# Two layers of a hybrid decoder on one core: value blocks that run ahead of a way down are convolved and gated inside it, and the FFN's short part is the last but one

## The chip, the cores and the metric

The kernel runs on one core of a Trainium2 chip. A core has five engines with instruction queues of their own, which meet only at semaphores: TensorE (PE) multiplies matrices, VectorE (DVE) and GpSimd (POOL) do elementwise work on two operands, ScalarE (ACT) does elementwise functions of one operand and issues some DMAs, SyncE (SP) issues DMAs. Each engine takes its queue strictly in the order in which it is written. Sums of products build up in PSUM, everything else lies in SBUF. The metric is the device time of one execution in microseconds (us).

## The reference

One inference step runs 512 prompt tokens and 8 x 4 sample tokens (544 columns in all) through two layers of width 1024: an even mixer (attention and linear attention), a ConvFFN, an odd mixer (short gated convolution), a ConvFFN. The change is in the ConvFFN, whose hidden width is 2816:

```python
def conv_ffn(h, w_up, conv_w, conv_b, w_down, past):
    u = h @ w_up                                   # 1024 -> 2 x 2816
    uc, new = causal_dwconv(u, past, conv_w)       # 3 taps along time
    gate, val = jnp.split(uc + conv_b, 2, axis=-1)
    return (jax.nn.gelu(gate, approximate=True) * val) @ w_down, new

# around every sub-layer f:
x = x + rmsnorm(f(rmsnorm(x, g_pre)), g_post)
```

Inputs and outputs are float32; the last two rows of `u` per sequence (`new`) are outputs too.

## The kernel before, in words

All activations lie transposed, features on partitions and the 544 tokens along the free axis, in two halves of 256 and 288 columns. For precision each product uses a weight W = wh + wl and an operand x = xh + xl and issues three matmuls, wh.xh, wh.xl and wl.xh (`mm3`, lines 280, 285, 287). Weights come as units of 128 x 512 floats by DMA on SP's queue; ACT rounds a unit to wh (L199) and DVE, in one place POOL, subtracts for wl (L203). Ten buffers hold wh and ten wl; eleven hold raw units. PSUM has five banks (`pg`) for the large products and three (`px`) for small ones.

**The FFN.** The 2816 hidden features are 22 gate blocks c and 22 value blocks FC + c of 128. Blocks 0 to 4 ("raw") are multiplied before the norm is known and scaled as they leave PSUM; block 5 is "plain"; blocks 6 to 21 come in `pair(c)` by a scheme of seven products for eight, whose weight sums POOL's accumulating DMAs make (L252, L256). When a block of u is complete, `conv(c)` saves the state rows (POOL), applies the taps (ACT L1702, DVE L1703 and L1704) and, for a gate, the gelu (ACT L1706); for a value block it multiplies by the gate (DVE L1711) and splits the product into `gh` (ACT L514) and `gl` (DVE L515), the operands of the way down.

**The way down** multiplies a run of blocks by `ffn_down` into eight output blocks m. `PARTS` lists the runs, and `ffn_order` sets them between the up-products: a way down starts when one block more than it uses has been multiplied ("runs ahead"), so that block's convolution and gating is issued ahead of it. With PARTS (4, 4, 4, 4, 4, 2) the order is raw 0-4, down 0-3, plain 5, pairs 6-8, down 4-7, pairs 9-12, down 8-11, pairs 13-16, down 12-15, pairs 17-21, down 16-19, down 20-21. Each result leaves PSUM in `Post.ev`: in the first way down ACT copies it to m (L592), later DVE adds it to m (L594). All but the last go block by block, both halves of a block together (`seq(8)`); the last does all first halves, then all second halves (`ALL8`), and squares each finished half (ACT L522, L526; sums on POOL, the eighth on DVE, L527). With the sum complete, `finish` computes the norm factor (PE L378, DVE L382, POOL L383, PE L390, ACT L393), scales m (L639), adds it to the residual (L643) and makes xh (ACT L645) and xl (DVE L653, L655) for the next layer; in the last layer `Final` writes the outputs instead, with transposes on PE (L181) and the norm factor late (PE L762, DVE L765, POOL L766, DVE L777).

**Work inside a way down.** `run` calls `tick` after each group, which takes one item off the list `work`. In the first way down the items are `normal(k)`, k = 0 to 3: they write the normed input xn (DVE L1724), split it into xh (ACT) and xl (DVE) for the later blocks, and form 16 sums of quarters on POOL (L1743 to L1746). `out_states` transposes the state rows (PE L181), copies them (ACT L1832) and writes them by DMAs on ACT's queue (L1834, L1836), at the start of the last way down.

The order in which each engine's instructions stand is set by a scheduler from the program's order and its own estimates, within the dependencies.

Of the kernel before, what the change touches and what calls it, by code (L numbers as in the profile page):

```python
# [29 lines left out]
F = 2816  # L30
FC = F // P
C2 = 2 * FC
PARTS = (4, 4, 4, 4, 4, 2)
RAW, PLAIN = 5, 6
UN = 4 * P
MID = T // 2
# [52 lines left out]
def tile_hybrid_step(  # L89
# [1559 lines left out]
    def odd_rows():  # L1649
        stT = cpool.tile([P, NB * 2 * 8], F32, tag="scT", name="scT")  # L1650
        to_cols(stT, *load_rows([(state_conv[0].rearrange("n i (c p) -> (n i c) p", p=P), P)]))
        early["odd"] = stT

    def ffn(l, xh, xl, bc, post):
# [8 lines left out]

        us = {}
        gs = {}

        def smp(t):
            return t[:, TP + 2 : TP + 2 + 6 * NB].rearrange("p (n k) -> p n k", k=6)

        def tv(t, t0=TP):  # L1670
            return t[:, t0 : t0 + TS].rearrange("p (n t) -> p n t", t=NT)

        def open_u(c):
            u = us[c] = tt(w=AW, s="u")
# [4 lines left out]
        def ev(c, scaled=True):  # L1679
            def f(hf, ps):  # L1680
                u = us[c] if c in us else open_u(c)
                if not scaled:
                    t0, n = HALF[hf]
                    S.activation(u[:, 2 + t0 : 258 + t0], ps[:, 0:256], AF.Copy)
                    if hf == 1:
                        S.activation(smp(u)[:, :, 2:6], tv(ps, 256), AF.Copy)
                        conv(c)
                    return
                if hf == 0:
                    V.tensor_tensor(u[:, 2:258], ps[:, 0:256], bc[:, 0:256], ALU.mult)  # L1690
                    return
                V.tensor_tensor(u[:, 258:514], ps[:, 0:256], bc[:, 256:512], ALU.mult)
                V.tensor_tensor(smp(u)[:, :, 2:6], tv(ps, 256), tv(bc), ALU.mult)
                conv(c)

            return f

# [63 lines left out]
        def pair(c):  # L1761

            h = slice(0, MID)
            pa, pb, pc, pd = bank(), bank(), bank(), bank()
            p1, p5, u2, u3 = ht(), ht(), ht(), ht()
            ua, ub = open_u(c), open_u(FC + c)
            product(pa, xq["11"], True)
            S.activation(p1[:, h], pa[:, h], AF.Copy)
            product(pb, xq["t2"], True)
            V.tensor_tensor(u2[:, h], p1[:, h], pb[:, h], ALU.subtract)  # L1770
            product(pc, xq["t1"], True)
            S.activation(p5[:, h], pc[:, h], AF.Copy)  # L1772
            product(pa, xq["21"], False)
            S.activation(ua[:, 2 : 2 + MID], pa[:, h], AF.Copy)
            product(pb, xq["t3"], False)
            V.tensor_tensor(u3[:, h], pb[:, h], p1[:, h], ALU.subtract)
            product(pc, xq["22"], False)
            n = TP - MID
            V.tensor_tensor(ua[:, 2 + MID : 2 + TP], pc[:, :n], u2[:, :n], ALU.add)
            V.tensor_tensor(smp(ua)[:, :, 2:6], tv(pc, n), tv(u2, n), ALU.add)  # L1780
            conv(c)
            product(pd, xq["t4"], True)
            G.tensor_tensor(ub[:, 2 + MID : 2 + TP], u3[:, :n], p5[:, :n], ALU.subtract)
            G.tensor_tensor(smp(ub)[:, :, 2:6], tv(u3, n), tv(p5, n), ALU.subtract)  # L1784
            V.tensor_tensor(ub[:, 2 : 2 + MID], u3[:, h], pd[:, h], ALU.subtract)
            conv(FC + c)

        work = []

        def tick():  # L1790
            if work:
# [2 lines left out]
        for kind, c0, n in ffn_order():  # L1794
            if kind == "raw":
                jobs = []
                for c in range(c0, c0 + n):
                    jobs += [(8, xh, xl, ev(c)), (8, xh, xl, ev(FC + c))]
                run(jobs, FIRST4 + seq(len(jobs) - 5, 5), spare=SPARE)
                work += [lambda k=k: normal(k) for k in range(4)]  # L1800
            elif kind == "plain":
                work += [lambda i=i: (parts(i), parts(i + 1), parts(i + 2)) for i in (0, 3)]
                run([(8, xh, xl, ev(c, False)) for c in (c0, FC + c0)], seq(2), tick=tick)
                for k in range(4):
                    last_operand(k)
            elif kind == "pair":
                pair(c0)
            else:
                last = c0 + n == FC
                gh = [gs[c][0] for c in range(c0, c0 + n)]  # L1810
                gl = [gs[c][1] for c in range(c0, c0 + n)]
                if last:
                    out_states(uc, ffn_p[l, 0].rearrange("i (c p) -> (i c) p", p=P),
                               ffn_s[l].rearrange("n i (c p) -> (n i c) p", p=P), 2 * C2)
                    if isinstance(post, Final):
                        post.begin()
                    else:
                        odd_rows()
                jobs = [(n, gh, gl, post.ev(m, c0 == 0, last)) for m in range(8)]
                run(jobs, ALL8 if last else seq(8), tick=tick)  # L1820

# [169 lines left out]
```

## Time and profile before

| | us |
|---|---|
| runs | 1351.59, 1348.55, 1353.99 (median 1351.59) |
| profiled execution: its own time | 1346.55 |
| its span in the trace | 1344.8 |
| PE busy | 1263.1 (94%), 9710 matmuls |
| DVE / ACT / POOL busy | 967.9 / 683.6 / 448.5 |

Times in the trace count from the span's start. Matmuls are pipelined, so a matmul of 0.28 us starts some 0.12 us after the one before it. A row of a timeline ends with the idle time before the instruction and what released it, in brackets, where the engine was idle. Idle time of an engine counts only where the end of the program hangs on it.

### The profile page before, as it was taken

What the parts mean: (1) busy time and instruction counts of PE and PEld (TensorE: products, weight loads), DVE (VectorE), ACT (ScalarE), POOL (GpSimd) and SP (SyncE); (2) the same over time, 40 slices, a digit from 0 to 9 for tenths busy, and PEclk for the clock granted to TensorE, in tenths of its full rate; (3) what the DMA queues carried; (4) which work ended last, traced back from release to release, by engine and by line L of the source; (5) the groups of instructions that cost most, each with busy time, mean ns of one, the idle gap of its engine ahead of it and who ended that gap; (6) DMA issues with size and microseconds to landing.
All of it is one profiled execution on the core that took longest, in us unless ns stands there. A gap on an engine that the chain in (4) does not pass through costs nothing.

```text
span 1344.8 us, 26495 instructions
## 1 busy us (share of the span) xinstructions
PE 1263.1 (94%) x9710; PEld 1222.5 (91%) x9710; DVE 967.9 (72%) x1958; ACT 683.6 (51%) x1489; POOL 448.5 (33%) x700
## 2 busy tenths in 40 slices
PE   8999989989899999989987999998979999999997
PEld 7999867889899999989977999998979999999996
DVE  7586465488959687878948655528886978787976
ACT  7554564655556364636634322335555646463634
POOL 4100210062463344445243100025254535353613
PEclk9999999999989999999988999999989999999998
DMA  8512220323657989989621332321456799989902
GB/s 255 128 47 61 86 71 10 89 64 97 130 105 185 185 195 185 219 173 219 173 66 32 111 90 86 92 79 32 131 114 140 182 194 205 193 197 196 214 8 74
DMA packets 311884, 171.98 MB, mean 128 GB/s; under 512 B 20829, under 2 KB 301882, under 8 KB 311738
## 3 DMA queue, kind: packets, MB, share of 16 engines
q1 hardware_dynamic: 262914, 132.17, 34.3%
q0 software_dynamic: 43456, 34.74, 18.1%
q10 hardware_dynamic: 5384, 3.38, 0.8%
q8 instruction: 76, 1.25, 0.4%
q14 instruction: 54, 0.44, 0.1%
HBM read 149.01 MB, written 5.47 MB: 115 GB/s over the span
## 4 chain that ended last, share of the span: by engine, by line
PE 70%; DMA 11%; DVE 9%; issue 5%; ACT 2%; POOL 2%; SPq 0%; POOLq 0%; DVEq 0%; ACTq 0%
PE pg L280 20%; PE pg L285 20%; PE pg L287 20%; DMA wr<-ffn_up 6%; DMA wr<-wr 4%; DVE m L639 2%; PE ps L181 2%; DVE xres L643 1%; PE ps L1075 1%; DVE wl L203 1%; PE ps L1408 1%; DVE xl L655 1%; PE ps L1347 1%; DVE xl L515 1%; PE ps L280 1%
## 5 line engine op out<-in xcount | busy, mean ns | idle before, releaser
L199 ACT ACTIVATE wh<-wr 128x512 fp32r<-128x512 f32 x478 | 295.5, 627 | 366.3 <-PE pg L285 302.9
L280 PE MATMUL pg<-xh,wh 128*128 128x256 f32 (+2 forms) x1536 | 438.5, 291 | 9.5 <-ACT h L1772 3.6
L203 DVE TENSOR_TENSOR wl<-wr,wh 128x512 fp32r<-128x512 f32 x466 | 340.0, 739 | 141.2 <-ACT wh L199 127.9
L285 PE MATMUL pg<-xl,wh 128*128 128x256 f32 (+2 forms) x1536 | 440.9, 289 | 0.7 <-DVE xl L518 0.7
L287 PE MATMUL pg<-xh,wl 128*128 128x256 f32 (+2 forms) x1520 | 435.7, 289 | 0.0
L280 PEld LDWEIGHTS pg<-xh,wh 128*128 128x128 f32 x1536 | 286.3, 189 | 14.7 <-ACT h L1772 5.0
L285 PEld LDWEIGHTS pg<-xl,wh 128*128 128x128 f32 x1536 | 289.7, 189 | 1.9 <-DVE xl L518 1.1
L287 PEld LDWEIGHTS pg<-xh,wl 128*128 128x128 f32 x1520 | 286.2, 189 | 1.3 <-issue 0.9
L280 PE MATMUL pg<-gh,wh 128*128 128x256 f32 (+1 forms) x704 | 205.1, 297 | 26.9 <-ACT m L592 15.1
L285 PE MATMUL pg<-gl,wh 128*128 128x256 f32 (+1 forms) x704 | 205.6, 294 | 0.0
L287 PE MATMUL pg<-gh,wl 128*128 128x256 f32 (+1 forms) x704 | 205.3, 294 | 0.0
L280 PEld LDWEIGHTS pg<-gh,wh 128*128 128x128 f32 x704 | 135.5, 195 | 28.9 <-ACT m L592 15.5
L285 PEld LDWEIGHTS pg<-gl,wh 128*128 128x128 f32 x704 | 136.9, 195 | 0.0
L287 PEld LDWEIGHTS pg<-gh,wl 128*128 128x128 f32 x704 | 136.3, 194 | 0.0
L256 POOL DMA_DIRECT2D wr<-ffn_up x64 | 94.2, 1471 | 108.7 <-DVE wl L203 43.2
L594 DVE TENSOR_TENSOR m<-m,pg 128x256 f32<-128x256 f32 (+1 forms) x176 | 73.0, 434 | 69.0 <-PE pg L287 68.8
L252 POOL DMA_DIRECT2D wr<-wr x64 | 58.0, 906 | 179.6 <-DMA wr<-ffn_up 40.8
L280 PE MATMUL pg<-qh,wh 128*128 128x272 f32 x384 | 110.0, 288 | 0.7 <-DVE h L1770 0.6
L285 PE MATMUL pg<-ql,wh 128*128 128x272 f32 x384 | 110.4, 288 | 0.0
L287 PE MATMUL pg<-qh,wl 128*128 128x272 f32 x384 | 110.2, 287 | 0.0
L1702 ACT ACTIVATE y<-u,cw 128x560 f32<-128x560 f32 x88 | 73.6, 850 | 48.3 <-POOL u L1784 37.3
L1703 DVE SCALAR_TENSOR_TENSOR y<-u,cw,y 128x560 f32<-128x560 f32 x88 | 73.5, 848 | 17.9 <-ACT y L1702 17.8
(327 smaller groups left out, 2265.6 us busy)
## 6 DMA issues: line engine op xcount, KB each, us to landing
wr<-ffn_up SPq DMA_DIRECT2D x272, 256.0 KB, 3.8
wr<-ffn_down SPq DMA_DIRECT2D x88, 256.0 KB, 4.0
wr<-ffn_up POOLq DMA_DIRECT2D x64, 256.0 KB, 5.8
wr<-wr POOLq DMA_DIRECT2D x64, 256.0 KB, 4.8
wr<-w_in_odd SPq DMA_DIRECT2D x48, 256.0 KB, 2.9
wr<-w_in_even SPq DMA_DIRECT2D x28, 256.0 KB, 4.3
wr<-w_out_odd SPq DMA_DIRECT2D x16, 256.0 KB, 2.6
xt<-x_prompt SPq DMA_DIRECT2D x8, 256.0 KB, 4.9
```

Source lines behind the costliest of these rows:

```text
L181: PE.transpose(out, in_, ident[:k, :k])
L199: ins = S.activation(wh, src, AF.Copy)
L203: ins = eng.tensor_tensor(wl, src, wh.bitcast(F32), ALU.subtract)
L252: in_turn("sum", G.dma_start(t[k], src, accum_op=ALU.add))
L256: in_turn("sum", G.dma_start(t[k].rearrange("p (k c) -> p k c", k=4), src, accum_op=ALU.add))
L280: ins = PE.matmul(ps[:, :n], lhsT=wh, rhs=xh[kb][:, sl], start=first, stop=False, skip_group_check=True)
L285: PE.matmul(ps[:, :n], lhsT=wh, rhs=xl[kb][:, sl], start=False, stop=last and packed, skip_group_check=True)
L287: PE.matmul(ps[:, :n], lhsT=wl, rhs=xh[kb][:, sl], start=False, stop=last, skip_group_check=True)
L594: V.tensor_tensor(self.m[m][:, sl], self.m[m][:, sl], ps[:, :n], ALU.add)
L639: chain(V.scalar_tensor_tensor(m, m, gcol(self.kind, self.l, c), self.bc[:, sl], ALU.mult, ALU.mult))
L1702: S.activation(y[:, 0:560], u[:, 2:562], AF.Identity, scale=cv(2, c), bias=cv(3, c))
L1703: V.scalar_tensor_tensor(y[:, 0:560], u[:, 1:561], cv(1, c), y[:, 0:560], ALU.mult, ALU.add)
```

## The change

`PARTS` becomes (4, 4, 4, 4, 2, 4): the two-block part is now down 16-17, behind pair 21 in block-by-block order, and the last way down has the four blocks 18-21. And `conv` of a value block that runs ahead (`lagging`: 4, 8, 12, 16, and 21) is put off: the next way down takes it up as an item of `work`, in the first behind the four `normal`s, in the others behind one empty item.

```diff
-PARTS = (4, 4, 4, 4, 4, 2)
+PARTS = (4, 4, 4, 4, 2, 4)
...
+        work = []
+        put_off = []
+        lagging = {sum(PARTS[:i]) for i in range(1, len(PARTS) - 1)} | {FC - 1}
+
+        def value(c):
+
+            if c in lagging:
+                put_off.append(lambda: conv(FC + c))
+            else:
+                conv(FC + c)
...
+        def convolve(c):
+            if c < FC:
+                conv(c)
+            else:
+                value(c - FC)
...
                     if hf == 1:
                         S.activation(smp(u)[:, :, 2:6], tv(ps, 256), AF.Copy)
-                        conv(c)
+                        convolve(c)
...
                 V.tensor_tensor(smp(u)[:, :, 2:6], tv(ps, 256), tv(bc), ALU.mult)
-                conv(c)
+                convolve(c)
...
             V.tensor_tensor(ub[:, 2 : 2 + MID], u3[:, h], pd[:, h], ALU.subtract)
-            conv(FC + c)
-
-        work = []
+            value(c)
...
                     else:
                         odd_rows()
+                if not work:
+                    work.append(lambda: None)
+                work += put_off
+                put_off.clear()
                 jobs = [(n, gh, gl, post.ev(m, c0 == 0, last)) for m in range(8)]
                 run(jobs, ALL8 if last else seq(8), tick=tick)
```

Line numbers behind `work` grow by 16: the taps L1702 to L1704 are L1718 to L1720 after, the gelu L1706 is L1722, the product L1711 is L1727, xn L1724 is L1740, the state copies L1832 are L1850.

**First way down, ACT.** In the rows of before, m681 to m683 are the first output blocks, y779 is block 4 (gate, then the gated product) and gh790 its split; in front of the first PSUM copy stands:

```order
L514 ACTIVATE xh623_3373<-xn808_4527 128x544
L199 ACTIVATE wh845_4737<-wr843_4734 128x512
L514 ACTIVATE xh620_3370<-xn815_4570 128x544
L514 ACTIVATE xh624_3374<-xn816_4574 128x544
L514 ACTIVATE xh621_3371<-xn825_4619 128x544
L514 ACTIVATE gh790_4433<-y779_4355 128x512
L514 ACTIVATE gh790_4433<-y779_4355 128x32
L592 ACTIVATE m681_3672<-pg795_4446 128x256
L592 ACTIVATE m681_3672<-pg796_4447 128x288
L514 ACTIVATE xh625_3375<-xn826_4623 128x544
L592 ACTIVATE m682_3673<-pg805_4495 128x256
```

After, gh768 is the split of block 3, y830 value block 4 and gh831 the split of block 4:

```order
L514 ACTIVATE gh768_4279<-y757_4201 128x512
L514 ACTIVATE gh768_4279<-y757_4201 128x32
L514 ACTIVATE xh620_3370<-xn812_4558 128x544
L514 ACTIVATE xh624_3374<-xn813_4562 128x544
L592 ACTIVATE m681_3672<-pg792_4434 128x256
L1722 ACTIVATE y779_4355<-y779_4355 128x560
L199 ACTIVATE wh840_4703<-wr838_4700 128x512
L592 ACTIVATE m681_3672<-pg793_4435 128x288
L199 ACTIVATE wh845_4737<-wr843_4734 128x512
L1718 ACTIVATE y830_4655<-u788_4422,cw559_3121 128x560
L199 ACTIVATE wh856_4787<-wr848_4768 128x512
```

and behind the copies of m682 to m685, in the same queue:

```order
L592 ACTIVATE m684_3675<-pg820_4579 128x256
L592 ACTIVATE m684_3675<-pg821_4580 128x288
L592 ACTIVATE m685_3676<-pg828_4626 128x256
L592 ACTIVATE m685_3676<-pg829_4627 128x288
L514 ACTIVATE gh831_4659<-y779_4355 128x512
L514 ACTIVATE gh831_4659<-y779_4355 128x32
L592 ACTIVATE m686_3677<-pg836_4672 128x256
```

The first copy now stands ahead of the gelu of gate 4, and gh of block 4 behind ten of the sixteen copies instead of ahead of all.

**First way down, DVE.** Before, gl of block 3 (gl769) stands ahead of the PSUM reads of value block 4 (u788) and of all xn:

```order
L203 TENSOR_TENSOR wl829_4634<-wr828_4632,wh830_4635 128x512
L515 TENSOR_TENSOR gl769_4280<-y757_4201,gh768_4279 128x512
L1704 SCALAR_TENSOR_TENSOR y779_4355<-u778_4348,cw559_3121,y779_4355 128x560
L515 TENSOR_TENSOR gl769_4280<-y757_4201,gh768_4279 128x32
L1690 TENSOR_TENSOR u788_4422<-pg786_4372,nbc635_3385 128x256
L1692 TENSOR_TENSOR u788_4422<-pg787_4373,nbc635_3385 128x256
L1693 TENSOR_TENSOR u788_4422<-pg787_4373,nbc635_3385 128x8x4
L203 TENSOR_TENSOR wl834_4668<-wr833_4666,wh835_4669 128x512
L1724 SCALAR_TENSOR_TENSOR xn797_4474<-xres0_90,gv_98,nbc635_3385 128x544
L1724 SCALAR_TENSOR_TENSOR xn798_4478<-xres4_94,gv_98,nbc635_3385 128x544
L1724 SCALAR_TENSOR_TENSOR xn807_4523<-xres1_91,gv_98,nbc635_3385 128x544
```

After, that gl stands here:

```order
L1719 SCALAR_TENSOR_TENSOR y779_4355<-u778_4348,cw559_3121,y779_4355 128x560
L203 TENSOR_TENSOR wl826_4622<-wr825_4620,wh827_4623 128x512
L515 TENSOR_TENSOR xl626_3376<-xn794_4462,xh618_3368 128x544
L1706 TENSOR_TENSOR u788_4422<-pg786_4372,nbc635_3385 128x256
L515 TENSOR_TENSOR xl630_3380<-xn795_4466,xh622_3372 128x544
L1708 TENSOR_TENSOR u788_4422<-pg787_4373,nbc635_3385 128x256
L1709 TENSOR_TENSOR u788_4422<-pg787_4373,nbc635_3385 128x8x4
L515 TENSOR_TENSOR xl627_3377<-xn804_4511,xh619_3369 128x544
L203 TENSOR_TENSOR wl834_4668<-wr833_4666,wh835_4669 128x512
L1740 SCALAR_TENSOR_TENSOR xn813_4562<-xres6_96,gv_98,nbc635_3385 128x544
L515 TENSOR_TENSOR xl631_3381<-xn805_4515,xh623_3373 128x544
L515 TENSOR_TENSOR gl769_4280<-y757_4201,gh768_4279 128x512
```

Four xn stand ahead of these rows, too; the reads of value block 4 and four xl have moved ahead of gl of block 3, and the taps of value block 4 follow nine to thirteen rows behind it.

In the three middle ways down the orders of ACT, DVE, POOL and PE are the same as before.

**The way down ahead of the last, DVE, FFN 0.** Before (four blocks), with y1567 and y1571 for gate and value 21, gl1573 for their split:

```order
L1704 SCALAR_TENSOR_TENSOR y1571_8535<-u1548_8389,cw559_3121,y1571_8535 128x560
L594 TENSOR_TENSOR m682_3673<-m682_3673,pg1576_8574 128x256
L594 TENSOR_TENSOR m682_3673<-m682_3673,pg1577_8575 128x288
L203 TENSOR_TENSOR wl1598_8762<-wr1597_8760,wh1599_8763 128x512
L1711 TENSOR_TENSOR y1567_8508<-y1567_8508,y1571_8535 128x560
L594 TENSOR_TENSOR m683_3674<-m683_3674,pg1578_8602 128x256
L594 TENSOR_TENSOR m683_3674<-m683_3674,pg1579_8603 128x288
L203 TENSOR_TENSOR wl1609_8827<-wr1608_8825,wh1610_8828 128x512
L515 TENSOR_TENSOR gl1573_8540<-y1567_8508,gh1572_8539 128x512
L515 TENSOR_TENSOR gl1573_8540<-y1567_8508,gh1572_8539 128x32
L594 TENSOR_TENSOR m684_3675<-m684_3675,pg1580_8630 128x256
L594 TENSOR_TENSOR m684_3675<-m684_3675,pg1581_8631 128x288
```

After (two blocks), value 21 is y1575 and the split gl1577:

```order
L594 TENSOR_TENSOR m684_3675<-m684_3675,pg1581_8595 128x288
L594 TENSOR_TENSOR m685_3676<-m685_3676,pg1582_8610 128x256
L594 TENSOR_TENSOR m685_3676<-m685_3676,pg1583_8611 128x288
L594 TENSOR_TENSOR m686_3677<-m686_3677,pg1584_8626 128x256
L1727 TENSOR_TENSOR y1567_8508<-y1567_8508,y1575_8567 128x560
L594 TENSOR_TENSOR m686_3677<-m686_3677,pg1585_8627 128x288
L203 TENSOR_TENSOR wl1611_8774<-wr1610_8772,wh1612_8775 128x512
L594 TENSOR_TENSOR m687_3678<-m687_3678,pg1586_8642 128x256
L203 TENSOR_TENSOR wl1616_8797<-wr1615_8795,wh1617_8798 128x512
L594 TENSOR_TENSOR m687_3678<-m687_3678,pg1587_8643 128x288
L594 TENSOR_TENSOR m688_3679<-m688_3679,pg1588_8658 128x256
L515 TENSOR_TENSOR gl1577_8572<-y1567_8508,gh1576_8571 128x512
L515 TENSOR_TENSOR gl1577_8572<-y1567_8508,gh1576_8571 128x32
```

The product of block 21 stands behind ten of the sixteen adds instead of four, and its gl behind fifteen instead of six.

**The same place, ACT.** Before, the gelu of gate 21 is followed by a weight copy and gh; the state copies (`so`) come 9 rows later. After:

```order
L1850 ACTIVATE so1591_8675<-ps1590_8674 88x128
L1850 ACTIVATE so1591_8675<-ps1590_8674 128x128 x3
L1850 ACTIVATE so1593_8689<-ps1592_8688 128x128 x2
L1850 ACTIVATE so1593_8689<-ps1592_8688 64x128
L361 DMA rows1594_8700<-state_conv 128x128
L1852 DMA ffn_p<-so1591_8675 88x128
L1854 DMA ffn_s<-so1591_8675 128x128 x3
L1854 DMA ffn_s<-so1593_8689 128x128
L1722 ACTIVATE y1567_8508<-y1567_8508 128x560
L1854 DMA ffn_s<-so1593_8689 128x128
L1854 DMA ffn_s<-so1593_8689 64x128
```

The seven state copies and six of the eight DMA issues now stand ahead of that gelu; gh of block 21 follows it by seven rows.

**The last way down, PE.** Each output block has 12 matmuls per half instead of 6; the first half's factor (L378) stands behind 24 second-half matmuls before and after. Matmuls of gl of block 21 stand at the end of the first four output blocks of the first half. Its eight weight units of four blocks are held from the first halves to the second (before: four units, each for two output blocks).

## Rows read from the trace of the kernel before

**Rows 1.** The page: busy time of each engine, and the chain that ended last.

```profile
PE 1263.1 (94%) x9710; PEld 1222.5 (91%) x9710; DVE 967.9 (72%) x1958; ACT 683.6 (51%) x1489; POOL 448.5 (33%) x700
...
PE 70%; DMA 11%; DVE 9%; issue 5%; ACT 2%; POOL 2%; SPq 0%; POOLq 0%; DVEq 0%; ACTq 0%
```

**Rows 2.** Timeline of PE: start, length, instruction, idle time before it and its releaser.

```profile
357.06 0.28 PE L280 MATMUL pg<-gh,wh 128*128 128x256 f32 x1
...
372.19 0.61 PE L280 MATMUL pg<-gh,wh 128*128 128x288 f32 x1 [7.55 <-ACT m L592]
...
1000.63 0.61 PE L280 MATMUL pg<-gh,wh 128*128 128x288 f32 x1 [7.52 <-ACT m L592]
```

**Rows 3.** Timeline of ACT at the first way down of FFN 0.

```profile
363.67 1.73 ACT L514 ACTIVATE xh<-xn 128x544 fp32r<-128x544 f32 x3
371.12 0.75 ACT L514 ACTIVATE gh<-y 128x512 fp32r<-128x512 f32 x2 [5.71 <-DVE y L1711]
```

**Rows 4.** Timeline of DVE before and in the first way down of FFN 0.

```profile
353.02 0.73 DVE L1711 TENSOR_TENSOR y<-y,y 128x560 f32<-128x560 f32 x1
...
359.79 3.56 DVE L1724 SCALAR_TENSOR_TENSOR xn<-xres,gv,nbc 128x544 f32<-128x544 f32 x5
...
365.23 1.99 DVE L515 TENSOR_TENSOR xl<-xn,xh 128x544 fp32r<-128x544 f32 x3
...
370.35 0.73 DVE L1711 TENSOR_TENSOR y<-y,y 128x560 f32<-128x560 f32 x1
```

**Rows 5.** Timeline of PE at the ends of FFN 0 and FFN 1.

```profile
695.78 1.01 PE L378 MATMUL ps<-ones,pss 128*128 128x1 f32 x4 [5.05 <-DVE pss L527]
...
704.05 0.86 PE L280 MATMUL pg<-xh,wh 128*128 128x256 f32 x5 [1.32 <-ACT xh L645]
...
725.25 1.01 PE L378 MATMUL ps<-ones,nss 128*128 128x1 f32 x4 [7.66 <-DVE nss L527]
...
1321.34 0.61 PE L378 MATMUL ps<-ones,pss 128*128 128x1 f32 x4 [2.24 <-DVE pss L527]
```

**Rows 6.** Windows from each restart: stretch, length, busy times (count), granted clock, DMA share, GB/s.

```profile
372.20:380.00 7.80, 7.80 (x43) 7.80 (x44) 2.39 (x5) 3.34 (x9) 7.72 (x9) 0.68 0.12 36
695.80:704.00 8.20, 6.93 (x32) 6.70 (x32) 3.85 (x10) 3.15 (x8) 3.16 (x5) 0.65 0.05 15
725.30:735.00 9.70, 9.70 (x51) 9.70 (x52) 7.02 (x14) 3.80 (x8) 2.98 (x5) 0.64 0.29 85
1000.60:1008.40 7.80, 7.77 (x44) 7.77 (x45) 3.76 (x5) 3.52 (x10) 7.72 (x10) 0.70 0.11 34
1321.40:1327.90 6.50, 6.50 (x40) 6.50 (x40) 2.44 (x8) 3.04 (x7) 2.52 (x4) 0.74 0.00 0
```

**Rows 7.** Groups of POOL from 371.7 to 388.5; three more lines with four sums each.

```profile
L1746 POOL TENSOR_TENSOR q<-qd,xn 128x272 f32<-128x272 f32 x4 | 4.4, 1250 | 0.2
```

**Rows 8.** Timeline of POOL at the end of FFN 0.

```profile
712.80 5.86 POOL L527 TENSOR_TENSOR nss<-nss,h 128x256 f32<-128x256 f32 x6 [4.16 <-ACT nss L522]
```

**Rows 9.** Timeline of DVE in and behind that stretch.

```profile
713.38 1.01 DVE L639 SCALAR_TENSOR_TENSOR m<-m,gv,pbc 128x288 f32<-128x288 f32 x1
...
719.33 0.51 DVE L639 SCALAR_TENSOR_TENSOR m<-m,gv,pbc 128x288 f32<-128x288 f32 x1
```

**Rows 10.** Timeline of DVE in the way down ahead of the last, FFN 0.

```profile
661.12 0.77 DVE L594 TENSOR_TENSOR m<-m,pg 128x256 f32<-128x256 f32 x2
```

**Rows 11.** Timeline of ACT and its DMA issues at the last way down, FFN 0.

```profile
682.25 1.82 ACTq L1836 DMA_DIRECT2D ffn_s<-so  x4
```

**Rows 12.** Timeline of PE at the end of the program.

```profile
1327.85 0.29 PE L287 MATMUL pg<-gh,wl 128*128 128x288 f32 x1
...
1332.87 0.29 PE L762 MATMUL pt<-ones,pss 128*128 128x1 f32 x1 [0.47 <-DVE pss L717]
```

**Rows 13.** Timeline of DVE at the end of the program.

```profile
1338.72 0.69 DVE L746 COPY o<-pt 128x512 f32<-128x512 f32 x1 [1.14 <-PE pt L181]
```

**Rows 14.** Timeline of ACT and its DMA issues at the end of the program.

```profile
1341.46 0.34 ACTq L778 DMA_DIRECT2D y_prompt<-xt  x1
```


## Prediction

> **What bounds the kernel now.** I read the page first: TensorE (PE) is busy 94% of the span, and PE's work is the longest part of the chain that ended last, with the DMAs second at 11% [rows 1]. The 9,710 matmuls stay as they are, so the only time to be had is PE's idle time and the time it spends at the lower of its two clock levels (1.2 of 2.4 GHz). I then read the list of PE's waits, which names who ended each, PE's own timeline at the long ones, and last the granted clock of the stretch behind each. The reader is to see three kinds of place.
>
> First way down of each FFN: PE issues 60 matmuls into its five PSUM banks from 357.06, stops at 364.64, and starts again at 372.19, 7.55 us later; the second FFN shows the same with 7.52 us [rows 2]. The copy that would empty a bank stands on ScalarE (ACT) behind the gh of value block 4, and ACT itself has stood idle for 5.71 us until VectorE (DVE) delivers that block's product [rows 3]. DVE is never idle there: it works off seven xn, seven xl, the two convolution steps of value block 4 and then the product, which starts at 370.35 [rows 4]. So a block that the first way down doesn't use holds its PSUM copies.
>
> End of FFN 0: waits of 5.05 us (sums of squares of the first half), 1.32 us (first xh of the next layer) and 7.66 us (squares of the residual) [rows 5]. End of FFN 1: 2.24 us for the first of these [rows 5], and a tail of 16.65 us from the end of the last matmul at 1328.15 to the span's end at 1344.8 [rows 12].
>
> Behind each long wait the clock is at the lower level for some microseconds. Length times (1 - granted clock) is what that costs: 7.8 x 0.32 = 2.5 us, 7.8 x 0.30 = 2.3, 8.2 x 0.35 = 2.9, 9.7 x 0.36 = 3.5, 6.5 x 0.26 = 1.7 [rows 6].
>
> **Term 1: both first ways down.** By the order of instructions, gh and gl of block 4 move behind the copies of five output blocks, and the first PSUM copy moves ahead of the gelu of gate 4. In the three middle ways down nothing moves on ACT, DVE or PE, so value blocks 8, 12 and 16 cost and bring nothing; the no-op in the work list is no instruction. No instruction is added in this place; what goes is 7.55 + 2.5 = 10.1 us, and 7.52 + 2.3 = 9.8 us.
>
> What comes is the next late thing. I lay DVE's new order from 353.02 on, with the old durations: xn 3.56/5 = 0.71, xl 1.99/3 = 0.66, product 0.73 [rows 4], and a convolution step taken like the product. Seventeen instructions, among them six xn, the product of block 3 and three PSUM reads of value block 4, stand ahead of gl of block 3, which is then there at about 364.0. PE gets to it after some 50 matmuls of 7.58/60 = 0.126 us, at 363.3: 0.7 us of waiting. ACT's first copy follows at once, and the third stands behind a weight copy and two xh, whose xn is late on DVE: 1.7 us of waiting for banks together. GpSimd (POOL) now has its 16 sums, up to 1.25 us each [rows 7], beside DVE's dense stretch instead of behind it. While POOL adds squares [rows 8] one form of DVE instruction takes 1.01 us, and beside an idle POOL 0.51 [rows 9]: some ten two-input instructions could meet it, so the price is 0 to 5 us. I take 1.0, as most of POOL's sums wait for xn until DVE is through with the dense part. Lower clock behind these short waits: 0 to 2.5, I take 0.8. Together 4.2, so net -5.9 and -5.6, in sum -11.5 us, with -17 (hardly any of it arrives) and -4 (the upper prices) as ends.
>
> The Trainium skill bears on that price ("SBUF — State Buffer", section "Who interferes with whom"): a DVE instruction with two SBUF inputs and a GpSimd instruction that reads SBUF share a read port, and one waits for the whole of the other. The doubled row [rows 9] agrees. By that rule taken to its end the sum would lose the 5 us in each FFN instead of 1, which is rival 1 below.
>
> **Term 2: end of FFN 0.** The last way down has four blocks instead of two, so an output block has 12 matmuls (1.5 us) per half instead of 6 (0.75). The squares, some 0.8 us each on POOL, then keep pace, so the last sum ends an add, a square and a sum behind the last first-half matmul, some 2 us, and the 24 second-half matmuls that stand ahead of the rstd matmul, as before, cover 3.0. State copies and their DMA issues, which held up the squares on ACT, move ahead of the pass. So the 5.05 goes, with its 2.9 of clock. The way from rstd to xh lies beside a second pass of 12 us instead of 6, so the 1.32 goes, and most of apply(0) leaves the stretch that ends in 7.66 + 3.5. Goes: 5.05 + 2.9 + 1.32 + 7.66 + 3.5 = 20.4 us.
>
> Comes: (a) the short way down now stands where the long one was. It lasts 96 x 0.126 = 12.1 us for 16 PSUM adds of 0.77/2 = 0.39 [rows 10], the convolutions of gate and value 21 and four weight lows: about 11.4 us on DVE for 12.1 on PE. I take 1.6 us of waits, between 0 and 7. Block 21's gelu stands on ACT behind seven state copies and six DMA issues of 1.82/4 = 0.46 us [rows 11], together some 4.5 us; DVE comes to its product some 2.8 us after that, which hides it. (b) The second half's rstd: its squares now end 1.5 us later than PE's other work. (c) apply(1), 24 instructions of 0.51 to 1.01 us [rows 9] or some 17 us on DVE, starts behind the last add, and PE has 96 first-half matmuls, 12 us, to lie over it: about 5 us of waiting and 2.7 of clock stay. Together 10.8, net -9.6, ends -14 and -3. Weights of the next layer: eight instead of four of the ten split buffers are held to the second pass, each comes free 1.5 us after the one before. The odd mixer's first four columns want eight units, four of them from these buffers; I cost that at nothing while the 12 us pass covers it, and at up to 4 us if not.
>
> **Term 3: end of FFN 1.** Goes 2.24 + 1.7 of clock. In the tail, 4.7 us lie between the last matmul and the rstd matmul at 1332.87 [rows 12], in which DVE mixes apply(0) with the last adds; an add, a square and a sum alone are about 1.5, so 3.2 go. Copies that wait 1.14 us for transposes [rows 13] move forward, and residual transposes into the pass: 1.4. The last DMA issue at 1341.46 [rows 14] and the 3.3 us behind it stay. Comes: 1.6 for the short way down, and 1.5 for adds that lag behind the scaling on DVE. Net -(3.9 + 3.2 + 1.4) + 3.1 = -5.4 us, ends -7.5 and -1.
>
> **Sum.** -11.5 - 9.6 - 5.4 = -26.5 us. The profiled execution took 1346.55 us (span 1344.8), so 1320.0; the median of the runs, 1351.59, is 5.04 above it, so I forecast 1325.
>
> **Rivals.**
> 1. Term 1 is given back: POOL's sums stretch DVE's dense part by 5 us, or the pairs, whose chain runs over DMAs, start no earlier because their weights come when they came. For it: the doubled row [rows 9] and DMA's 11% of the chain [rows 1]. Against: in the stretch from 372.2 to 380 DMA is busy only 0.12 [rows 6], so loads can start earlier when buffers do. Time: 1351.6 - 15 = 1336.6.
> 2. The ends give nothing: the short way down is paced by DVE, each short wait brings the lower clock, and weights for the odd mixer come late. For it: 11.4 us of DVE work in 12.1. Against: DVE idles now through most of the last way down. Time: 1351.6 - 11.5 = 1340.
> 3. The change does nothing that counts, since DVE, busy throughout the first way down, only permutes what is late: 1350.
> 4. Slower. The one mechanism is block 21 in the short way down. ACT takes its queue in order, so gelu 21 waits for the state copies, whose transposes wait in turn for PE and for POOL's copy; DVE takes its queue in order too, so the PSUM adds behind block 21's product wait with it, the five banks stay full, and PE stands. Price: PE's wait beyond the 2.8 us of cover, plus up to 5 us of clock behind it, in each FFN. It decides when that is above 13 us per FFN, which takes a chain of some 11 us more than I lay: serial, the state work (4.5), weight copies (2.6) and convolution (8) come to 15 beside 12 of PE's. For it: both engines' new orders. Against: the product comes after twelve other DVE instructions. Time: 1360.
>
> **Chances.** The forecast 0.58, rival 1 0.20, rival 2 0.11, rival 3 0.05, rival 4 0.06. What a measurement of this kernel can tell from no change is about 0.5%, 6.8 us, so faster means under 1344.8 and slower above 1358.4. The forecast, rival 1 and four fifths of rival 2 are faster: 0.87; the rest of rival 2 and rival 3 the same: 0.07; rival 4: 0.06. The forecast's own range is 1312 (terms at -17, -13 and -7, which is -37, and 2.6 us for the scatter) to 1333. The range given reaches over rivals 1 and 2 to 1341 and leaves out rivals 3 and 4 and the outer ends of the terms.
>
> **What would show it.** Term 1: PE's wait of 7.5 us for the PSUM copy is gone in both FFNs, waits up to 1 us stand in its place, the granted clock stays up, and gh of block 4 lies behind PSUM copies on ACT. Term 2: no wait above 1 us for the first half's squares, DVE full in the short way down, and a wait of some 5 us in place of 7.66. Term 3: no 2.24 us wait, and a tail of about 12 us. It would be wrong if PE waits in the short way down for DVE's adds by more than 3 us, if gl of block 3 comes later than 365, or if waits for weights in the pairs grow by what the first way down saves.

## The result

The changed kernel takes 1328.12 us (median of 1325.54, 1327.93, 1328.32, 1329.8), the one before 1350.67 in the same comparison. The ratio is 0.9829, 95% interval 0.9803 to 0.9856: 23.1 us faster, where 26.5 were forecast. The profiled execution took 1325.54 us with a span of 1323.7, 21.1 less than before.

The page after, as in [rows 1]: busy times of the engines and the chain that ended last.

```profile
PE 1254.7 (95%) x9710; PEld 1214.5 (92%) x9710; DVE 981.0 (74%) x1958; ACT 682.6 (52%) x1489; POOL 449.5 (34%) x700
...
PE 71%; DVE 10%; DMA 8%; issue 6%; ACT 3%; POOL 2%; SPq 0%; POOLq 0%; DVEq 0%; ACTq 0%
```

PE's busy time is 8.4 us less for the same 9,710 matmuls, so less of it lies at the lower clock; the other 12.7 us are idle time. To see where the time went, I cut both spans at PE's matmuls on gh, at the same points of the program (a first way down lasts from its first such matmul to the end of its last):

| stretch | before | after | difference | forecast |
|---|---|---|---|---|
| start to the first way down, FFN 0 | 357.06 | 357.27 | +0.2 | |
| first way down, FFN 0 | 34.23 | 31.41 | -2.8 | -5.9 |
| from there to the way down before the last | 265.79 | 265.16 | -0.6 | 0 |
| from there through the odd mixer to FFN 1 | 328.41 | 318.13 | -10.3 | -9.6 |
| first way down, FFN 1 | 34.10 | 30.92 | -3.2 | -5.6 |
| from there to the way down before the last | 264.82 | 265.74 | +0.9 | 0 |
| from there to the end of the span | 60.39 | 55.07 | -5.3 | -5.4 |

The differences add up to -21.1. The ends of both FFNs give what was forecast, the first ways down half of it.

**First way down.** PE's timeline, FFN 0 and then FFN 1, to be held against [rows 2]:

```profile
364.05 0.39 PE L285 MATMUL pg<-gl,wh 128*128 128x256 f32 x1 [0.42 <-DVE gl L515]
...
372.74 0.61 PE L280 MATMUL pg<-gh,wh 128*128 128x288 f32 x1 [4.18 <-ACT m L592]
...
987.33 0.40 PE L280 MATMUL pg<-gh,wh 128*128 128x288 f32 x1 [4.06 <-ACT m L592]
```

The short wait for gl of block 3 is there, 0.42 us. The wait for the PSUM copy is not gone, it is 4.18 and 4.06 us instead of 7.55 and 7.52. ACT's timeline shows what the copy stands behind now, against [rows 3]:

```profile
368.55 0.85 ACT L1718 ACTIVATE y<-u,cw 128x560 f32<-128x560 f32 x1 [1.68 <-POOL qd L1761]
...
370.56 0.66 ACT L514 ACTIVATE xh<-xn 128x544 fp32r<-128x544 f32 x1 [0.64 <-DVE xn L1740]
371.76 0.66 ACT L514 ACTIVATE xh<-xn 128x544 fp32r<-128x544 f32 x1 [0.55 <-DVE xn L1740]
372.32 0.94 ACT L592 ACTIVATE m<-pg 128x256 f32<-128x256 f32 x3
```

ACT waits for a buffer that POOL's sums still read, then twice for an xn from DVE, and only then copies. DVE's timeline, against [rows 4], has no idle time in this stretch, but instructions that take several times their length:

```profile
366.00 5.73 DVE L1740 SCALAR_TENSOR_TENSOR xn<-xres,gv,nbc 128x544 f32<-128x544 f32 x2
...
378.25 1.75 DVE L1720 SCALAR_TENSOR_TENSOR y<-u,cw,y 128x560 f32<-128x560 f32 x1
...
380.53 3.64 DVE L1727 TENSOR_TENSOR y<-y,y 128x560 f32<-128x560 f32 x1
```

Two xn take 5.73 us together where five took 3.56 before (the first alone takes 4.53); DVE's second tap of value block 4 takes 1.75 and the product 3.64 instead of 0.73. Over the first xn POOL runs four sums, each starting before the one ahead has ended; the xn gets through behind the first gap, from 369.93 to 370.01:

```profile
366.47 1.32 POOL L1759 TENSOR_TENSOR qd<-xn 128x272 f32<-128x272 f32 x1
367.22 2.00 POOL L1761 TENSOR_TENSOR qd<-xn,xn 128x272 f32<-128x272 f32 x2
368.68 1.25 POOL L1760 TENSOR_TENSOR qd<-xn,qd 128x272 f32<-128x272 f32 x1
370.01 1.14 POOL L1762 TENSOR_TENSOR q<-qd,xn 128x272 f32<-128x272 f32 x1
```

What kept them out of the way before was POOL's own queue: the memset of a buffer for u stood ahead of the sums and waited for DVE's product of value block 4, so that they began at 371.81. In the trace of before:

```profile
371.14 0.10 POOL L1675 MEMSET u<- 128x2 f32 x1 [1.64 <-DVE y L1711]
371.81 1.28 POOL L1743 TENSOR_TENSOR qd<-xn 128x272 f32<-128x272 f32 x1
```

After, that memset stands behind nine of the sums, at 375.86.

Behind each restart the clock still falls to 1.2 GHz for some of the time, against [rows 6]; the row in the middle is the stretch behind the squares of the residual at the end of FFN 0:

```profile
372.70:380.50 7.80, 7.76 (x45) 7.76 (x46) 7.80 (x8) 2.41 (x7) 7.22 (x9) 0.70 0.54 136
...
713.40:723.10 9.70, 9.68 (x63) 9.68 (x64) 9.11 (x18) 6.51 (x16) 4.71 (x5) 0.82 0.01 3
...
987.30:995.10 7.80, 7.77 (x49) 7.77 (x50) 7.80 (x8) 2.94 (x9) 7.14 (x9) 0.78 0.54 134
```

**Ends.** PE's waits from 650 to 730, the end of FFN 0 (in all, times, longest), against the 5.05, 1.32 and 7.66 of [rows 5]:

```profile
PE ps L378 <- DVE nss L527: 3.3, 1, 3.3
PE pg L280 <- DVE m L594: 1.6, 1, 1.6
PE pg L280 <- DVE u L1801: 1.2, 1, 1.2
PE ps L378 <- DVE pss L527: 0.8, 1, 0.8
PE ps L390 <- POOL r L383: 0.3, 1, 0.3
```

No wait for the first half's squares is left; the 0.8 us is one for the second half's, and the 1.2 us lies in the short way down. At the end of FFN 1 the 2.24 us wait is gone too, and the tail has changed, against [rows 12, 14] (PE's norm factor, then the last DMA issue on ACT's queue):

```profile
1308.49 0.30 PE L287 MATMUL pg<-gh,wl 128*128 128x288 f32 x1
...
1311.92 0.60 PE L762 MATMUL pt<-ones,pss 128*128 128x1 f32 x4 [0.26 <-DVE pss L717]
...
1317.32 0.33 ACTq L778 DMA_DIRECT2D y_prompt<-xt  x1
```

From the last matmul on gh, which ends at 1308.79, to the norm factor it is 3.1 us instead of 4.7, and to the last DMA issue 8.5 instead of 13.3. But the span ends 6.4 us behind that issue, where it was 3.3, so the tail is 14.9 us instead of 16.65.

### The profile page after: what moved, and what is told of

Its sections match the earlier page's. It is cut to its first block, busy times and chain, and to the rows that moved or that the text cites. A ratio compares the mean times of both kernels' runs of the same rounds, so it can differ in the third digit from the quotient of the medians.

```text
span 1323.7 us, 26494 instructions
## 1 busy us (share of the span) xinstructions
PE 1254.7 (95%) x9710; PEld 1214.5 (92%) x9710; DVE 981.0 (74%) x1958; ACT 682.6 (52%) x1489; POOL 449.5 (34%) x700
## 4 chain that ended last, share of the span: by engine, by line
PE 71%; DVE 10%; DMA 8%; issue 6%; ACT 3%; POOL 2%; SPq 0%; POOLq 0%; DVEq 0%; ACTq 0%
PE pg L280 21%; PE pg L285 20%; PE pg L287 20%; DMA wr<-ffn_up 4%; DVE m L639 2%; DMA wr<-wr 2%; DVE xres L643 2%; PE ps L181 2%; DVE wl L203 1%; PE ps L1075 1%; PE ps L1408 1%; DVE xl L655 1%; PE ps L1347 1%; DVE xn L1740 1%; PE ps L280 1%
## 5 line engine op out<-in xcount | busy, mean ns | idle before, releaser
L203 DVE TENSOR_TENSOR wl<-wr,wh 128x512 fp32r<-128x512 f32 x466 | 334.0, 727 | 126.6 <-ACT wh L199 114.5
L280 PE MATMUL pg<-gh,wh 128*128 128x256 f32 (+1 forms) x704 | 202.4, 295 | 21.3 <-DVE m L594 10.6
L256 POOL DMA_DIRECT2D wr<-ffn_up x64 | 96.9, 1515 | 114.6 <-DMA wr<-ffn_up 26.9
L1718 ACT ACTIVATE y<-u,cw 128x560 f32<-128x560 f32 x88 | 73.6, 851 | 44.0 <-POOL u L1800 32.2
```

Source lines behind the costliest of these rows:

```text
L203: ins = eng.tensor_tensor(wl, src, wh.bitcast(F32), ALU.subtract)
L256: in_turn("sum", G.dma_start(t[k].rearrange("p (k c) -> p k c", k=4), src, accum_op=ALU.add))
L280: ins = PE.matmul(ps[:, :n], lhsT=wh, rhs=xh[kb][:, sl], start=first, stop=False, skip_group_check=True)
L1718: S.activation(y[:, 0:560], u[:, 2:562], AF.Identity, scale=cv(2, c), bias=cv(3, c))
```

## Experiments

Each was compared with the kernel before on its own chip; the ratios, not the medians, are to be compared.

### The two halves of the change, each alone

```diff
-PARTS = (4, 4, 4, 4, 2, 4)
+PARTS = (4, 4, 4, 4, 4, 2)
...
-        lagging = {sum(PARTS[:i]) for i in range(1, len(PARTS) - 1)} | {FC - 1}
+        lagging = {4}
```

> The put-off of value block 4 alone, with the parts of before. If the two traces read rightly, the first way down gains 2.8 us in FFN 0 and 3.2 us in FFN 1 and nothing else moves: the ratio to before is about 0.9955 (6 us). Rival: the pairs behind it are paced by DMAs and take that back, ratio 0.999 or more. PE's wait for the PSUM copy is about 4.2 us in both FFNs under either.

Measured: ratio 0.9946 (0.9926 to 0.9966), 7.3 us. PE's wait for the copy is 4.29 and 3.22 us. The rival falls: the pairs don't take it back.

```diff
-        lagging = {sum(PARTS[:i]) for i in range(1, len(PARTS) - 1)} | {FC - 1}
+        lagging = set()
```

> The new parts alone, no block put off. If the traces read rightly, the ends of the two FFNs gain 10.3 and 5.4 us and the 7.5 us waits of the first ways down stay: the ratio to before is about 0.988 (15.7 us), and the two halves of the change add up to the whole. Rival: the ends need the put-off of block 21; then the ratio is 0.992 or above, with waits for gl of block 21 in the last way down.

Measured: ratio 0.9905 (0.9875 to 0.9936), 12.8 us, with the old waits of 7.55 and 7.52 us in the first ways down and the new ones (1.67, 0.77, 3.33 us) at the end of FFN 0. PE waits nowhere for gl of block 21, so the rival falls. The two halves come to 0.54% and 0.95%, 1.49% together, where the whole gives 1.71% (1.44% to 1.97%): they add up within what can be told. By the order of instructions the put-off of block 21 moves nothing on ACT, DVE or PE in the end of the FFN, so nothing but the put-off of block 4 in the first ways down stands for its half.

### What holds the first way down: POOL's sums made twice

```diff
-            G.tensor_tensor(u[:, lo_h], xa[:, lo_h], xa[:, hi_h], ALU.subtract)
+            for _ in range(2):
+                G.tensor_tensor(u[:, lo_h], xa[:, lo_h], xa[:, hi_h], ALU.subtract)
...
```

The other three sums of `normal` stand in the same loop.

> The changed kernel, with each of POOL's 16 sums in the first way down made twice (same result). Theory (POOL's back-to-back sums keep DVE's two-operand instructions from starting): the xn that took 4.53 us takes 7 us or more, PE's wait for the copy grows from 4.2 us to 7 or more in both FFNs, and the time grows by 5 to 12 us, to 1333 to 1340. Rival (DVE is late by its own load, POOL only fills the gaps): the wait stays at 4 to 5 us and the time within 3 us of 1328.

Measured: ratio 0.9965 (0.9945 to 0.9986), that is some 18 us slower than the change, more than expected. The timelines of DVE, ACT and PE in the first way down of FFN 0, the two xn, the xh made of them, and PE's restart behind its wait:

```profile
366.52 10.22 DVE L1740 SCALAR_TENSOR_TENSOR xn<-xres,gv,nbc 128x544 f32<-128x544 f32 x2
```

```profile
376.07 1.35 ACT L514 ACTIVATE xh<-xn 128x544 fp32r<-128x544 f32 x2 [7.87 <-DVE xn L1740]
```

```profile
377.75 0.61 PE L280 MATMUL pg<-gh,wh 128*128 128x288 f32 x1 [8.66 <-ACT m L592]
```

The two xn take 10.22 us instead of 5.73, and PE waits 8.66 us (8.50 in FFN 1) instead of 4.2. POOL's doubled work, not DVE's own, sets the wait. It isn't a wait for a buffer: here ACT waits for xn alone, and the first tap of value block 4, which had waited for a buffer in the change, stands behind the copies. The first ways down last 8.2 us longer in all, and the stretches behind them, up to the second ways down, another 10.9 us: the pairs there multiply what the sums make.

### The copies ahead on ACT

```diff
...
+            self.copies = []
...
-                    S.activation(self.m[m][:, sl], ps[:, :n], AF.Copy)
+                    self.copies.append(S.activation(self.m[m][:, sl], ps[:, :n], AF.Copy))
...
+            if c == FC + 4 and len(post.copies) >= 6:
+                behind(ins, post.copies[5])
...
+            if c % 4 == 3 and len(post.copies) >= 6:
+                behind(ins, post.copies[5])
```

The first `if` stands in `conv`, behind the first tap on ACT, the second in `normed`, behind the xh of k = 3.

> The changed kernel, with the copies of m1 to m3 ahead of the last two xh and of the first tap of value block 4 on ACT; POOL's sums stay where they are. Theory (queue position): PE's 4.2 us wait is there because the copies stand behind xh, whose xn is held up on DVE; it falls to under 1 us in both FFNs, the granted clock stays up, and the time falls by 8 to 11 us, to about 1318, although one xn on DVE still takes some 4.5 us. Rival (DVE's lateness reaches PE in another way, by gl of block 3 or by weight lows): another wait of 3 us or more takes its place and the time stays within 3 us of 1328.

Measured: ratio 0.9858 (0.9812 to 0.9903), no gain that can be told. In FFN 0 the longest wait of the first way down is 1.14 us, but that is no test of the theory, which expected an xn of 4.5 us: here the two xn take only 2.52 us together.

```profile
366.16 2.52 DVE L1744 SCALAR_TENSOR_TENSOR xn<-xres,gv,nbc 128x544 f32<-128x544 f32 x2
```

POOL's second sum starts only as the first ends there, and the two engines take turns. In FFN 1 the two xn take 5.69 us. The copies ahead of them are through and PE doesn't wait there, as the theory says, but the wait comes back further on, as the rival says, as 5.43 us. The rows of FFN 1, DVE, ACT and PE:

```profile
988.36 1.67 DVE L203 TENSOR_TENSOR wl<-wr,wh 128x512 fp32r<-128x512 f32 x1
989.95 2.95 DVE L1724 SCALAR_TENSOR_TENSOR y<-u,cw,y 128x560 f32<-128x560 f32 x1
992.94 1.17 DVE L1731 TENSOR_TENSOR y<-y,y 128x560 f32<-128x560 f32 x1
```

```profile
994.15 0.75 ACT L514 ACTIVATE gh<-y 128x512 fp32r<-128x512 f32 x2 [8.74 <-DVE y L1731]
994.80 0.37 ACT L594 ACTIVATE m<-pg 128x256 f32<-128x256 f32 x1
```

```profile
995.22 0.61 PE L280 MATMUL pg<-gh,wh 128*128 128x288 f32 x1 [5.43 <-ACT m L594]
```

Now it is DVE's second tap (2.95 us) and the product (1.17) of value block 4 that come late beside POOL's sums; gh waits for them 8.74 us on ACT, and the copies of m6 stand behind gh. The place in ACT's queue alone is not the answer, since the lateness finds the next instruction that comes from DVE.

### POOL's sums later

```diff
+            pending.append((k, xa, xb))
+            if k == 3:
+                for i in (3, 0, 1, 2):
+                    sums(*pending[i])
```

`sums` holds the four lines of POOL; the first sum in its queue needs the last xn.

> The changed kernel, with POOL's 16 sums issued from the last k on, so that the first of them waits for the last xn on DVE; the work is the same, and the scheduler also sets the first ways down's products anew. Theory (POOL's sums starve DVE, late xn holds ACT, ACT holds PE's banks): the seven other xn and the last two run at some 0.8 us each, PE's wait of 4.2 us behind the first copies falls under 1 us, and the time falls by 5 us or more, to 1323 or less. The starving then meets the convolution of value block 4, so that a wait of up to 5 us can come back at the copies behind its gh, as in the run with the copies first; then the time stays near 1328.

Measured: ratio 0.9797 (0.9762 to 0.9833), 4.3 us below the change by the ratios, with intervals that meet: not to be told from it by time. DVE's timeline at the same place as in the rows above:

```profile
366.07 1.47 DVE L1740 SCALAR_TENSOR_TENSOR xn<-xres,gv,nbc 128x544 f32<-128x544 f32 x2
...
374.55 4.38 DVE L1720 SCALAR_TENSOR_TENSOR y<-u,cw,y 128x560 f32<-128x560 f32 x1
...
380.86 6.01 DVE L203 TENSOR_TENSOR wl<-wr,wh 128x512 fp32r<-128x512 f32 x1
```

The two xn take 1.47 us instead of 5.73, with the same instructions ahead of them on DVE: beside them only POOL was taken away. DVE's second tap (4.38) and a weight low (6.01 instead of 0.68) take the blow instead, as was expected. PE's wait behind the first copies is gone, one of 1.42 and 1.40 us stands further on, at 382.04 and 991.95, and the first ways down last 26.5 and 26.6 us. PE's products and ACT's copies stand in another order here, so that this is not POOL's doing alone. The stretches behind them, up to the second ways down, last some 1.5 us longer each, which takes a third of the gain back.

### Value block 4 behind the last copy

The run with the copies ahead, and value block 4 gated behind the last of the sixteen copies:

```diff
-            if c == FC + 4 and len(post.copies) >= 6:
-                behind(ins, post.copies[5])
+            if c == FC + 4 and len(post.copies) >= 16:
+                behind(ins, post.copies[15])
...
-                if not work:
-                    work.append(lambda: None)
+                work += [lambda: None] * (3 if c0 == 0 else 1 - len(work))
                 work += put_off
```

> The changed kernel, with the copies of m1 to m3 ahead of the last two xh, and the convolution and gating of value block 4 put off behind the last copy of the first way down. POOL's sums stay. Theory (PE waits only where a copy stands on ACT behind something that comes from DVE): no wait over 1 us is left in both first ways down though DVE is starved as before; they last 25 to 27 us (31 with the change), and the time falls by 8 to 10 us against the change, to 1318 to 1320. Rival (the pairs behind are paced by DMAs): the first ways down shorten as said, but less than half of it is left at the end, 1324 or more.

Measured: ratio 0.9748 (0.9717 to 0.9779), 10.9 us better than the change, with intervals that don't meet. The windows of the two first ways down, in the columns of [rows 6], and two rows of DVE's timeline in the first:

```profile
358.70:383.60 24.90, 24.50 (x196) 24.30 (x195) 24.90 (x27) 13.53 (x32) 17.45 (x19) 1.00 0.42 95
972.00:997.00 25.00, 24.53 (x196) 24.33 (x195) 25.00 (x27) 13.47 (x32) 17.44 (x18) 1.00 0.44 93
```

```profile
367.44 5.73 DVE L1744 SCALAR_TENSOR_TENSOR xn<-xres,gv,nbc 128x544 f32<-128x544 f32 x2
...
379.08 7.49 DVE L203 TENSOR_TENSOR wl<-wr,wh 128x512 fp32r<-128x512 f32 x4
```

DVE is starved as in the change (5.73 us for two xn, 7.49 for four weight lows), yet PE is busy for 24.50 of 24.90 us at the full clock. The longest wait left is one for gl, 0.4 us in FFN 0 and 0.5 in FFN 1. Two xh still stand between the sixth and the seventh copy, and ACT waits 1.72 and 0.56 us for their xn, but PE doesn't wait there. The rival falls: what the first ways down gain is there at the end.

Both at once, the sums late as well:

> The run before, with POOL's sums from the last k on as well. If PE waits for nothing from DVE in the first ways down any more, the starving no longer counts, and this is the same as the run before within 3 us. If lows of weights on DVE still hold PE, this is 3 us or more faster.

Measured: ratio 0.9735 (0.9704 to 0.9767), the same as the run before within what can be told. DVE is held less here: its two xn take 1.47 us, and one weight low of the first way down 1.90. Once block 4 stands behind the copies, the starving costs nothing that shows.

### POOL's weight lows at the end of a layer

```diff
-                prepare(nxt[0] + 7, G)
+                prepare(nxt[0] + 7)
```

> The changed kernel, with the weight lows that POOL makes behind each layer's first half done on DVE instead. By the starving theory DVE's scaling and adding of the first half (L639, L643), which take up to 1.5 us beside POOL's lows, fall to 0.4 to 0.5 us, PE's wait of 1.65 us at the start of the odd mixer goes, and the time falls by 1 to 4 us although DVE has more to do. Rival (DVE's load decides there): the lows cost DVE 0.6 us each in the stretch that PE waits for, the wait grows to 3 us or more, and the time rises by 1 to 5 us.

Measured: ratio 0.9814 (0.9782 to 0.9845), not to be told from the change. The theory is right about PE's wait of 1.65 us at the odd mixer's start, which is gone, but the time doesn't show it, and the wait for the squares of the residual is longer:

```profile
718.03 0.59 PE L378 MATMUL ps<-ones,nss 128*128 128x1 f32 x2 [5.46 <-DVE nss L527]
```

5.46 us instead of 3.33. The run doesn't say why: the last sum of squares also stands behind fourteen of DVE's instructions on the second half here, instead of eleven. Waits elsewhere changed as well (5.32 us in the first way down of FFN 0, 3.33 us in the pairs at 641.99), so that the time alone prices the lows neither way.

### The tail

```diff
-            nc.scalar.dma_start(y_sample.rearrange("n t (q d) -> q (n t) d", q=4), self.xs)
+            nc.sync.dma_start(y_sample.rearrange("n t (q d) -> q (n t) d", q=4), self.xs)
```

> The changed kernel, with the write of the sample rows issued on SP's queue instead of ACT's. In every run with the new parts the span ends 4.4 to 6.4 us after the last DMA issue, in those with the old parts 3.4 us. Theory: the last write of the prompt stands on ACT's queue right behind the sample write, issued 0.9 us before it; with that write on the other queue the distance falls to 3.4 to 4 us. Rival: the six last writes share the same DMA engines whatever queue they are issued on, so the distance stays at 4.4 to 6.4. In time either is within 3 us of the changed kernel, less than can be told.

Measured: ratio 0.9843 (0.9796 to 0.9890); the span ends 5.5 us behind the last issue. The theory falls. With everything together:

> The kernel with the copies first, the gating of value block 4 behind the last copy, POOL's sums from the last k on, and the sample write on SP's queue. No wait over 1 us in either first way down; the ratio to before is 0.970 to 0.976, about 1315 us. If the sample write matters, the span ends 3.4 to 4 us after the last DMA issue here as well.

Measured: ratio 0.9757 (0.9721 to 0.9792), again no wait over 1 us in the first ways down, and again 5.4 us behind the last issue. It is no faster than the two runs without that last edit. A row of the windows after and one of before show what differs:

```profile
1318.00:1319.20 1.20, 0.00 (x0) 0.00 (x0) 0.00 (x0) 0.00 (x0) 0.00 (x0) 1.00 0.39 64
```

```profile
1338.60:1340.00 1.40, 1.33 (x6) 0.71 (x4) 1.28 (x3) 0.32 (x1) 0.00 (x0) 0.57 0.33 98
```

The last six writes are issued within 3.8 us, before within 4.2, so that they come hardly closer together. But in each trace there is a stretch behind the write of the sample rows in which the DMAs move little, 64 and 98 GB/s. Before, that write is issued 3.8 us ahead of the last issue, and the stretch lies ahead of the last three issues; after, it is issued 0.9 us ahead, and the stretch lies behind the last issue. That this write makes the stretch is not shown: the run with it on the other queue issues it just as late, and no run issues it earlier.

## Why the prediction was right, and where it was not

**Time, direction and range.** 1328.1 lies inside 1312 to 1341 and within the likeliest case's own range, 3 us from the 1325 forecast. That it is so near is in part luck. The profiled execution misses its 1320.0 by 5.5 us, which is the half of term 1 that didn't come; the median lies 2.6 us above it, where 5.04 was added.

**Term 1: half its size.** What goes was right, 10.1 and 9.8 us. The step that failed is the price of POOL's sums beside DVE's dense stretch, "I take 1.0, as most of POOL's sums wait for xn until DVE is through with the dense part". They don't: before, they waited in POOL's queue behind a memset, and with that out of their way and six xn moved forward they start at 366.47, before the last two xn are through, and the two take 5.73 us instead of 1.4. That is 4.3 us on one pair of instructions, near the upper end of 0 to 5 for the whole way down. The bound had been laid by one form taken twice as long [rows 9], but in these runs a DVE instruction was held for as long as POOL's sums overlapped. The end of -4 had been called the upper prices, but their sum, 0.7 + 1.7 + 5 + 2.5 = 9.9, leaves next to nothing of 10.1 and 9.8. The third copy stands behind just these xn, so "1.7 us of waiting for banks" came to 4.18, and the clock cost 7.8 x 0.30 = 2.3 us instead of 0.8. Arrivals were 0.42 + 4.18 + 2.3 = 6.9 us, not 4.2, and 10.1 - 6.9 = 3.2 is near the 2.8 measured. Rival 1 named this mechanism; it took about half of the term rather than all of it. By the rule of the Trainium skill ("SBUF — State Buffer", section "Who interferes with whom") one of the two engines waits for the whole of the other's instruction. The runs agree on the pair, since the two xn take 1.47 us with POOL moved away, and in FFN 0 of the run with the copies ahead the two engines did take turns, but here the hold goes beyond one instruction: 4.3 us is more than three of POOL's sums of 1.3 us.

I had not counted buffers either: ACT waits 1.68 us for one for the first tap of value block 4, as it seems because eight xn and two other blocks fill the ten of their kind until POOL has read an xn. But this wait sets nothing, since ACT waits again behind it for both xn, and the copies stand behind the second.

**Term 2: right in size, by other parts, which is luck in part.** The 5.05 us wait and its clock went as forecast. The 1.32 us wait did not go: 1.65 us stand in its place, for adds of the second half that lie on DVE behind scaling that POOL's lows hold up. Of the arrivals, 1.23 (short way down, 1.6 forecast), 0.77 + 0.30 (second rstd, 1.5) and 3.33 with 9.7 x 0.18 = 1.7 of clock (7.7 forecast) came smaller. Together 9.0 with the 1.65, for 10.8 forecast; the stretch gave 10.3 us for a forecast 9.6. The 11.4 us of DVE's work in the short way down were too few: 6.2 for the adds, 3.65 for four convolution steps and a product and some 2.4 for the lows make 12.3, and DVE is busy through all 14.2 us from 653.8 to 668.0; that PE waits only 1.23 us there is less than such a load would suggest. Block 21 was covered as said: gelu 21 ends at 663.6, DVE takes up its product at 665.37, 1.7 us later, where I had 2.8. Rivals 2 and 4 had the right places, and no price there came near theirs.

**Term 3: the sum was right, two parts were not.** Up to the last matmul on gh the end gained 3.6 us, more than the 2.3 that 3.9 - 1.6 leaves. From there to the last issue it gained 4.8, where 3.2 + 1.4 less the lag of 1.5 was forecast. But the outputs' DMAs gave 3.0 of that back. The step that failed is "The last DMA issue at 1341.46 [rows 14] and the 3.3 us behind it stay", and that the sum still came out is luck. The other runs say the same: the span ends 3.4 us behind the last issue with the old parts, and 4.4 to 5.8 in the nine runs with the new.

**The middle.** The pairs' stretches differ by -0.6 and +0.9 us with the same order of instructions, so nothing is read into them.

## What to carry to other kernels

Moving work on a busy engine is not free of its neighbours: ask not only what the engine does in its dense stretch, but what another engine will now run beside it, and count how many such instructions can follow one another. Look also at what had kept the other engine's work away, here one instruction ahead of it in its own queue. Where an engine in the middle (here ACT) empties PSUM, let nothing stand ahead of a copy that can be later than the free banks cover; here that gave 10.9 us, while moving the disturbance elsewhere gave 4.3, not to be told from none. And when a tail of work gets shorter, look at what lies behind its last instruction, here the output writes, whose slow stretch came to lie behind the last issue.

## What the runs showed of the hardware that was not expected

A DVE instruction with two operands in SBUF was held for as long as POOL's sums overlapped, each starting some 0.7 us after the one before: two xn, 1.47 us by themselves, took 5.73 beside the sums and 10.22 beside doubled sums, and a weight low of 0.68 took 6.01. It goes the other way too. In the run with the sums late, POOL's first sum, elsewhere 0.8 to 1.4 us long, lasts from 367.00 to 371.26, over five DVE instructions of their usual length that follow one another without a gap:

```profile
367.00 4.26 POOL L1767 TENSOR_TENSOR qd<-xn 128x272 f32<-128x272 f32 x1
```

Where a sum started only when the one ahead had ended, the two engines took turns and the two xn took 2.52 us. So in these runs the engine whose instructions followed one another without a gap kept the other out until a gap came; why they overlap in one place and not in another stays open. The time of a held instruction shows as busy, not as idle, so that no list of waits names it; only the mean of a form, or its length beside the same form elsewhere, gives it away.
